# Layer 0's attention begins with heads 0 and 1, later key and query tiles run beside head 0, and values stay in SBUF

## The chip, the cores and the metric

The kernel runs on one core of one Trainium2 chip, as one launch. The metric is the device time of the launch in microseconds (us). The engines are named as the profile names them: PE is TensorE (PEld its weight loads), DVE is VectorE, ACT is ScalarE, POOL is GpSimd and SP is SyncE, which issues all DMA transfers of this kernel in one queue. SBUF is the memory on the core, DRAM the memory beside it.

## The reference

One inference step of a two-layer network over 1024 latent and 128 context tokens, 1024 channels wide. Layer 0 is what this case is about; layer 1 (a neighbourhood attention) and the feed-forward parts follow.

```python
def mla_split(h, w_in, ...):
    a_in, q_lat, kv_lat, k_rope = split(h @ w_in, (512, 768, 896), axis=-1)
    q = (rms_norm(q_lat, q_lora_norm) @ w_q_up).reshape(B, S, 8, 96)    # 64 plain + 32 rotary channels a head
    q = rms_norm(q, mla_q_norm)                                          # over the 96 channels of each head
    ckv = rms_norm(kv_lat, kv_lora_norm)
    return a_in, q, ckv, k_rope

def mla_keys_values(ckv, k_rope, w_kv_up, mla_k_norm):
    kv = (ckv @ w_kv_up).reshape(B, L, 8, 64 + 64)
    k_nope, v = kv[..., :64], kv[..., 64:]
    k = concatenate([k_nope, broadcast_to(k_rope, every head)], axis=-1)
    return rms_norm(k, mla_k_norm), v

def pool_mla_latent(h, ckv_ctx, krope_ctx, ...):
    ...
    q, k = rope_tail(q), concatenate([rope_tail(k_lat), k_ctx], axis=1)
    v = concatenate([v_lat, v_ctx], axis=1)                              # 1024 + 128 keys
    attn = softmax(q @ k.T * 96 ** -0.5) @ v                             # 8 heads
    return concatenate([pool_mixer(a_in, w_pool, pool_scale), attn], axis=-1) @ w_out
```

Context tokens run the same projections and attend to context tokens alone (`pool_mla_context`). `pool_mixer` subtracts each channel from a windowed mean and multiplies four groups of 128 channels by a 128x128 matrix each. Beside this a modulation is computed for each layer, silu(c) @ w_ada + b_ada, 6 x 1024 values from a 1024 x 6144 matrix.

## The kernel before, in words

**Precision.** An f32 product is made of three matmuls: each operand is split into a high half (a cast on ACT) and a low half (the operand less its high half), and low·high, high·low and high·high add up in one PSUM tile. So each tile of keys or queries exists as a high and a low tile.

**Stages of layer 0 around the change.** The in-projection and the query chunks (`query_chunk`, three pieces of 384 tokens) leave raw keys and queries of all heads as channel-by-token tiles: four tiles of plain channels with two heads each (tiles 0 to 3) and two of rotary channels with four heads each (tiles 4 and 5). `key_tile(t)` and `query_tile(t)` finish a tile: PE spreads the norm's factors over the partitions (`bcast`, L682 and L683, two matmuls with 8 rows into PSUM tile `ps_b`), DVE multiplies with them (L758 and L779 among others), and `split_store` casts the high half `fh` on ACT, subtracts on POOL for the low half (L691) and stores both to DRAM (`qdn`, `qdr`, `kdn`, `kdr`). Tiles run in the order 4, 0, 5, 1, 2, 3. A head needs one plain and one rotary tile: head 0 needs 0 and 4, heads 2 and 3 need 1 and 4, heads 4 to 7 need 5 with 2 or 3. `load_qk(h)` brings a head's high halves back as 96-row tiles `qh` and `kh`, `load_rest(h)` the low halves `ql` and `kl` and the head's values.

After the tiles comes one block: `max_units` of heads 0 and 1, woven with `value_gen` (values, stored to DRAM as `vd`, ten steps), `context_gen0` (attention of the context tokens) and `mix_gen` (the pooling mixer, L826 its vector part `pl`).

**Maxima.** The softmax subtracts a maximum for each query. `max_units(h)` computes the scores once in low precision: 24 matmuls of 96x384 (L1034), each reduced by DVE (L1035). Then `put_max` reduces the 24 columns to 8 (L1016), transposes them on PE (`ps_mt`, L1020), and sends the row through DRAM: `row` to `mrow` and `mrow` to row 96 of `qh`. Row 96 of `kh` holds ones, so that the third matmul of a score (L1074, 97 rows) subtracts the maximum by itself. Of a head's scores only L1074 needs the maxima; the first two (L1070, L1073) don't.

**The heads.** Each head has two halves of 512 queries, each with nine key tiles: three matmuls into `ps_st`, an exponential on ACT into `p`, and the product with the values (`ps_pv`, L1077), one key tile's scores being issued ahead of an earlier one's product. At a half's end DVE copies the result out (L1001). Beside head h run the maxima of head h + 2, and the modulation (`ada_gen`: a load of `wada`, a reduction with `silu` on DVE, L200) as background work that the head calls twice a half, from head 0 on.

**What sets the order.** Python generators are interleaved by `weave`, which always takes the next step of the generator that is least far along by its weight; the numbers beside the generators are these weights. A scheduler behind it then sorts each engine's instructions by its own estimate of when each can run, under data dependences and one added rule (`LAG`): a score isn't started before the maximum that lies four maxima back in the program. Each engine runs its list strictly in order, so an instruction that waits holds all behind it. SBUF is given out in slots by a small allocator (`S`); PSUM tiles come from three tags, with three buffers for `ps_st`, three shared by maxima, broadcasts and small work, two for the products.

## Time and profile before

| | |
|---|---|
| median of 3 runs | 3011.77 us (3011.28 to 3014.54) |
| the profiled execution's own time | 3018.45 us |
| its span in the trace | 3016.6 us |
| PE busy | 2914.8 us, 97% |
| PEld busy | 2612.8 us, 87% |
| DVE busy | 2149.4 us, 71% |
| ACT busy | 1331.9 us, 44% |
| POOL busy | 306.9 us, 10% |
| DMA | 372 MB, mean 123 GB/s |
| share of the chain that ended last | PE 80%, DVE 6%, DMA 6%, issue 5% |

The times below are from the span's start. The stretch that the change touches runs from the tiles, at about 231 us, to the end of head 7, at 576.2 us. In the profile's rows a number after `L` is the line, the letters before it the engine, then operation, output and inputs. Rows of a group end with the time busy and the mean of one in ns, then the idle time ahead of them and what ended it. Rows of the timeline begin with the start and the length in us. `SPq` is a transfer, at the time at which SP issued it. PEclk is the clock that PE was granted, as a share of the full one, and a windows row gives it after the engines.

### The profile page before, as it was taken

The page shows a single profiled execution, that of the slowest core. Times are in us where ns is not written, and L with a number is a line of the kernel's source. Part 1 is how long each engine was busy: PE and PEld are TensorE (multiplying, and loading weights), DVE is VectorE, ACT ScalarE, POOL GpSimd, SP SyncE. Part 2 cuts the span into 40 slices and gives each one's busy share as a digit, 9 for nine tenths or more (in the row PEclk, how much of TensorE's full clock was granted, in tenths as well). Part 3 has the DMA queues.
Part 4 walks back from the last instruction along what each step waited for, and adds up shares of the span by engine and source line. Part 5 has one row for each costly group of instructions (what it writes and reads, how often), then busy time and mean ns, then how long its engine had stood idle before and what let it go on. Part 6 is the DMA issues. An engine that isn't in the chain of part 4 may idle for free.

```text
span 3016.6 us, 46513 instructions
## 1 busy us (share of the span) xinstructions
PE 2914.8 (97%) x18302; PEld 2612.8 (87%) x18302; DVE 2149.4 (71%) x3921; ACT 1331.9 (44%) x2177; POOL 306.9 (10%) x210
## 2 busy tenths in 40 slices
PE   7998899999999999999999999998989999999999
...
PEclk9996899999999999999999999998999999999999
...
GB/s 234 169 62 306 212 61 50 77 76 86 99 84 85 105 133 147 85 99 80 173 187 223 126 146 208 185 240 155 101 29 98 79 97 85 116 100 78 98 76 87
DMA packets 148268, 372.37 MB, mean 123 GB/s; under 512 B 14225, under 2 KB 67073, under 8 KB 148050
## 3 DMA queue, kind: packets, MB, share of 16 engines
...
## 4 chain that ended last, share of the span: by engine, by line
PE 80%; DVE 6%; DMA 6%; issue 5%; ACT 2%; POOL 1%; SPq 0%; DVEq 0%; POOLq 0%; ACTq 0%
PE ps L452 9%; PE ps L454 9%; PE ps L453 9%; PE ps L422 8%; PE ps L424 8%; PE ps L423 8%; PE ps_n L335 2%; PE ps_n L336 2%; PE ps_n L337 2%; PE ps_pv L1329 2%; PE ps_o L335 1%; PE ps_o L336 1%; PE ps_o L337 1%; PE ps_pv L1077 1%; PE ps_v L1353 1%
## 5 line engine op out<-in xcount | busy, mean ns | idle before, releaser
L452 PE MATMUL ps<-ml,wh 128*128 128x288 f32 x2048 | 592.3, 296 | 10.3 <-DVE ml L441 7.8
L453 PE MATMUL ps<-mh,wl 128*128 128x288 f32 x2048 | 601.3, 295 | 0.0
L454 PE MATMUL ps<-mh,wh 128*128 128x288 f32 x2048 | 597.0, 295 | 0.0
L422 PE MATMUL ps<-bl,wh 128*128 128x288 f32 x1792 | 532.8, 298 | 13.3 <-DVE bl L353 10.3
L423 PE MATMUL ps<-bh,wl 128*128 128x288 f32 x1792 | 529.7, 296 | 0.0
L424 PE MATMUL ps<-bh,wh 128*128 128x288 f32 x1792 | 528.2, 295 | 0.0
L452 PEld LDWEIGHTS ps<-ml,wh 128*128 128x128 f32 x2048 | 381.5, 188 | 11.3 <-DVE ml L441 8.3
L453 PEld LDWEIGHTS ps<-mh,wl 128*128 128x128 f32 x2048 | 385.5, 188 | 0.0
L454 PEld LDWEIGHTS ps<-mh,wh 128*128 128x128 f32 x2048 | 383.6, 188 | 0.1
L458 DVE SCALAR_TENSOR_TENSOR x<-ps,ada,x 128x288 f32<-128x288 f32 (+2 forms) x640 | 270.0, 451 | 119.1 <-PE ps L454 117.8
L422 PEld LDWEIGHTS ps<-bl,wh 128*128 128x128 f32 x1792 | 336.8, 188 | 16.7 <-issue 11.5
L424 PEld LDWEIGHTS ps<-bh,wh 128*128 128x128 f32 x1792 | 338.4, 189 | 0.0
L423 PEld LDWEIGHTS ps<-bh,wl 128*128 128x128 f32 x1792 | 337.5, 188 | 0.2
L395 ACT CAST wh<-s 128x512 fp32r<-128x512 f32 x256 | 146.1, 618 | 305.8 <-PE ps L454 217.1
L160 ACT CAST wh<-wr 128x1024 fp32r<-128x1024 f32 x188 | 196.9, 1050 | 176.4 <-PE ps L424 79.9
L200 DVE CUSTOM_DVE_ANT_0 trash<-wada,silu 128x1024 bf16<-128x1024 f32 x160 | 203.2, 1270 | 28.0 <-DMA wada<-in_wada0t 16.4
L161 DVE TENSOR_TENSOR wl<-wr,wh 128x1024 fp32r<-128x1024 f32 x144 | 179.6, 1251 | 46.6 <-ACT wh L160 46.5
L395 ACT CAST wh<-wr 128x1024 fp32r<-128x1024 f32 (+1 forms) x128 | 106.9, 835 | 220.5 <-PE ps L454 155.4
L161 POOL TENSOR_TENSOR wl<-wr,wh 128x1024 fp32r<-128x1024 f32 x44 | 119.3, 2718 | 701.9 <-ACT wh L160 686.2
L396 DVE TENSOR_TENSOR wl<-s,wh 128x512 fp32r<-128x512 f32 x232 | 157.1, 710 | 3.5 <-ACT wh L395 1.2
L1278 DVE CUSTOM_DVE_ANT_0 trash<-ps_m,ta 128x512 bf16<-128x512 f32 (+1 forms) x128 | 83.4, 651 | 100.7 <-PE ps_m L1276 91.9
L1035 DVE TENSOR_REDUCE stat<-ps_m 128x1 f32<-128x384 f32 x192 | 99.3, 551 | 77.8 <-PE ps_m L1034 77.4
...
## 6 DMA issues: line engine op xcount, KB each, us to landing
wr<-in_w SPq DMA_DIRECT2D x256, 512.0 KB
...
```

The source lines that it names most:

```text
L160: nc.scalar.copy(hi, r)
L161: (nc.gpsimd if e else nc.vector).tensor_sub(lo, r, hi)
L200: nc.vector.tensor_tensor_reduce(trash, r[:, :D], silu[i][:, :D], scale=1.0, scalar=0.0, op0=ALU.mult, op1=ALU.add, accum_out=a)
L395: nc.scalar.copy(h, src)
L396: (nc.gpsimd if j in EDGE and min(ps) in EDGE_POOL else nc.vector).tensor_sub(l, src, h)
L422: nc.tensor.matmul(ps, wh[:, a], hl[:, b], start=k == 0, stop=False)
L423: nc.tensor.matmul(ps, wl[:, a], hh[:, b], start=False, stop=False)
L424: nc.tensor.matmul(ps, wh[:, a], hh[:, b], start=False, stop=k == 3)
L452: nc.tensor.matmul(ps, wh, hl, start=kk == 0, stop=False)
L453: nc.tensor.matmul(ps, wl, hh, start=False, stop=False)
L454: nc.tensor.matmul(ps, wh, hh, start=False, stop=kk == 3)
L458: nc.vector.scalar_tensor_tensor(x[m][:, a:b], ps[:, a - ch * HC:b - ch * HC], g, x[m][:, a:b], op0=ALU.mult, op1=ALU.add)
```

## The change

Three things are changed, and the diff below shows them, with unchanged lines left out at "...".

**Values.** `vd` and its loads are gone. `value_gen` writes each token tile's values, in two pieces by ACT, straight into six SBUF tiles `vt` (three for heads 0 to 3, three for 4 to 7) in the layout that the product reads, whose columns of ones POOL writes once. `head_values0` gives the piece for a key tile and head.

**Order ahead of head 0.** Key and query tiles became generators that take the engine of their subtraction: DVE for tiles 4 and 0, POOL as before for the others. Tiles 4 and 0 run first, then head 0's loads, then a block of head 0's maxima, the values and tile 1, then head 1's high loads. Head 0 starts behind it.

**Beside the heads.** Head 0 runs beside head 1's maxima and `rest_gen`: tiles 5 and 2, the low loads of head 1, the high loads of head 2, tile 3. Head 1 runs beside head 2's maxima and the mixer, head 2 beside head 3's maxima and the context tokens, each later head beside the maxima of the next one, not of the one after it. The modulation starts with head 2 and is called three times a half. Copies of the context's results move to heads 4 and 6.

```diff
--- before.py
+++ after.py
@@ -524,7 +524,6 @@
 
     qd_n, qd_r = [DR(f"qdn{i}", [4, P, NS]) for i in range(2)], [DR(f"qdr{i}", [2, P, NS]) for i in range(2)]
     kd_n, kd_r = [DR(f"kdn{i}", [4, P, TOK]) for i in range(2)], [DR(f"kdr{i}", [2, P, TOK]) for i in range(2)]
-    vd0 = DR("vd0", [9, P, 768], F32)
 
 
...
@@ -684,11 +683,11 @@
 
...
-    def split_store(raw, ncols, dst, i):
+    def split_store(raw, ncols, dst, i, eng):
         hi, lo = S.alloc("fh", F32R), raw.bitcast(F32R)
         c = slice(0, ncols)
         nc.scalar.copy(hi[:, c], raw[:, c])
-        nc.gpsimd.tensor_sub(lo[:, c], raw[:, c], hi[:, c])
+        eng.tensor_sub(lo[:, c], raw[:, c], hi[:, c])
...
         S.free(hi)
@@ -746,7 +745,7 @@
                 nc.vector.tensor_add(tq[t - 2][:, cs], tq[t - 2][:, cs], sw)
...
-    def key_tile(t):
+    def key_tile(t, eng):
         raw = tk[t] if t < 4 else S.alloc("kro")
         for ch in range(NCH):
             ps = PS("ps_b", "pb")[:, :CH]
@@ -758,16 +757,18 @@
                     nc.vector.scalar_tensor_tensor(o, raw[:, a:b], V("kn_nope"), pp_, op0=ALU.mult, op1=ALU.mult)
                 else:
                     nc.vector.tensor_mul(o, krr[:, a:b], pp_)
+            yield
...
         if t < 4:
             nc.vector.scalar_tensor_tensor(raw[:, NS:], tkc[:, t * P:t * P + P], V("kn_nope"), ps, op0=ALU.mult, op1=ALU.mult)
         else:
             nc.vector.tensor_mul(raw[:, NS:], kr4c, ps)
-        split_store(raw, TOK, kd_n if t < 4 else kd_r, t if t < 4 else t - 4)
+        split_store(raw, TOK, kd_n if t < 4 else kd_r, t if t < 4 else t - 4, eng)
         S.free(raw)
-
-    def query_tile(t):
+        yield
+
+    def query_tile(t, eng):
         raw = tq[t]
         for ch in range(NCH):
             ps = PS("ps_b", "pb")[:, :CH]
@@ -779,24 +780,35 @@
                     nc.vector.scalar_tensor_tensor(o, raw[:, a:b], V("qn_nope"), pp_, op0=ALU.mult, op1=ALU.mult)
                 else:
                     nc.vector.tensor_mul(o, raw[:, a:b], pp_)
-        split_store(raw, NS, qd_n if t < 4 else qd_r, t if t < 4 else t - 4)
+            yield
+        split_store(raw, NS, qd_n if t < 4 else qd_r, t if t < 4 else t - 4, eng)
         S.free(raw)
+        yield
+
+    def tile_gen(t, eng):
+        yield from key_tile(t, eng)
+        yield from query_tile(t, eng)
 
     for ch in range(NCH):
         query_chunk(ch)
     S.free(*[t for p in qlat for t in p], rc, rs, nt)
     for t in (4, 0):
-        key_tile(t)
-        query_tile(t)
-    for t in (5, 1, 2, 3):
-        key_tile(t)
-        query_tile(t)
-    S.free(krr, *rk8, bcs)
+        run(tile_gen(t, nc.vector))
+
 
 
     vp = S.alloc("vp")
+    vt0 = [[S.alloc(f"vt{q}{i}") for i in range(3)] for q in range(2)]
+    v40 = [[t.rearrange("p (a e f) -> p a e f", e=3, f=64) for t in q] for q in vt0]
+
+    def head_values0(t, h):
+        o = t % 3 * 384 + h % 4 // 2 * 192 + h % 2 * 64
+        return vt0[h // 4][t // 3][:, o:o + P]
 
     def value_gen():
+        for q in v40:
+            for t in q:
+                nc.gpsimd.memset(t[:, :, 1], 1.0)
         for tt in range(10):
             ps = PS("ps_v")
             if tt < 9:
@@ -809,12 +821,12 @@
             if tt == 8:
                 nc.scalar.copy(vp[:, :512], ps)
             else:
-                vs = S.alloc("vst")
-                place_values(vs[:, :768], ps)
-                dma(vd0[min(tt, 8)], vs[:, :768])
-                S.free(vs)
+                t = min(tt, 8)
+                for q in range(2):
+                    nc.scalar.copy(v40[q][t // 3][:, t % 3 * 2:t % 3 * 2 + 2, 0:3:2],
+                                   ps[:, q * 256:q * 256 + 256].rearrange("p (g e f) -> p g e f", e=2, f=64))
             yield
-        S.free(*ckv, small)
+        S.free(*ckv)
...
@@ -977,14 +989,13 @@
         return qh, kh
 
     def load_rest(h):
-        ql, kl, v = S.alloc("ql", F32R), S.alloc("kl", F32R), S.alloc("v")
+        ql, kl = S.alloc("ql", F32R), S.alloc("kl", F32R)
         n0, r0 = 64 * (h % 2), 32 * (h % 4)
         dma(ql[0:64, :NS], qd_n[1][h // 2, n0:n0 + 64, :])
         dma(ql[64:96, :NS], qd_r[1][h // 4, r0:r0 + 32, :])
         dma(kl[0:64, :], kd_n[1][h // 2, n0:n0 + 64, :])
         dma(kl[64:96, :], kd_r[1][h // 4, r0:r0 + 32, :])
-        load_pv(vd0, h, v)
-        return ql, kl, v
+        return ql, kl
 
 
...
@@ -1055,8 +1066,7 @@
...
     def attend_units(h, qk, rest, opair, den):
-        (qh, kh), (ql, kl, vv) = qk, rest
-        v = vv.rearrange("p (t f) -> p t f", t=9)
+        (qh, kh), (ql, kl) = qk, rest
...
         for half in range(2):
...
@@ -1074,14 +1084,14 @@
...
                 nc.scalar.activation(p_, ps, AF.Exp, scale=scale0)
-                nc.tensor.matmul(po, v[:, kt, :], p_, start=kt == 0, stop=kt == 8)
+                nc.tensor.matmul(po, head_values0(kt, h), p_, start=kt == 0, stop=kt == 8)
...
                     held = None
                 if kt == 6:
                     later()
-                if kt in (2, 6):
+                if kt in (1, 4, 7):
                     background()
                 yield
             finish_values(64 * (h % 2), half, po, opair, den, half and h % 2)
@@ -1089,29 +1099,54 @@
 
     background(10 ** 6)
     S.free(*silu)
-    qks = {0: load_qk(0), 1: load_qk(1)}
-    weave((chain(max_units(0, qks[0]), max_units(1, qks[1])), 50), (chain(value_gen(), context_gen0()), 17),
-          (mix_gen(), 13))
-    rest = load_rest(0)
-    silu_load()
-    bg.append(chain(ada_gen(0, range(16 + 8 * NEARLY, 48)), free_silu()))
+    qks = {0: load_qk(0)}
+    rest = {0: load_rest(0)}
+    weave((max_units(0, qks[0]), 25), (value_gen(), 10), (tile_gen(1, nc.gpsimd), 7))
+    qks[1] = load_qk(1)
+
+
+    def rest_gen():
+        yield from tile_gen(5, nc.gpsimd)
+        yield from tile_gen(2, nc.gpsimd)
+        rest[1] = load_rest(1)
+        qks[2] = load_qk(2)
+        yield
+        yield from tile_gen(3, nc.gpsimd)
+        S.free(krr, *rk8, bcs, small)
+
     opairs = []
     for h in range(8):
         if h % 2 == 0:
             op, den = S.alloc(f"o{h}"), S.alloc("den")
             opairs.append(op)
-            nc.vector.tensor_copy(op[:, NS:], oat[:, (h // 2) * P:(h // 2) * P + P])
-        gs = [(attend_units(h, qks[h], rest, op, den), 19)]
+        if h == 2:
+            silu_load()
+            bg.append(chain(ada_gen(0, range(16 + 8 * NEARLY, 48)), free_silu()))
+        if h == 4:
+            for i in range(3):
+                nc.vector.tensor_copy(opairs[i][:, NS:], oat[:, i * P:i * P + P])
+        if h == 6:
+            nc.vector.tensor_copy(op[:, NS:], oat[:, 3 * P:4 * P])
+            S.free(oat)
+        gs = [(attend_units(h, qks[h], rest[h], op, den), 19)]
+        if 0 < h < 7:
+            rest[h + 1] = load_rest(h + 1)
+        if 0 < h < 6:
+            qks[h + 2] = load_qk(h + 2)
         if h < 7:
-            nrest = load_rest(h + 1)
-        if h < 6:
-            qks[h + 2] = load_qk(h + 2)
-            gs.append((max_units(h + 2, qks[h + 2]), 27))
+            gs.append((max_units(h + 1, qks[h + 1]), 31))
+        if h == 0:
+            gs.append((rest_gen(), 24))
+        elif h == 1:
+            gs.append((mix_gen(), 14))
+        elif h == 2:
+            gs.append((context_gen0(), 8))
         weave(*gs)
-        S.free(*qks[h], *rest)
-        rest = nrest
+        S.free(*qks[h], *rest[h])
+        if h == 3:
+            S.free(*vt0[0])
+    S.free(*vt0[1])
     later(2)
-    S.free(oat)
 
 
...
```

The rows that follow are the programs' instruction lists. Lines of the changed kernel have other numbers: L1045 and L1046 are the maxima and their reductions, L1080, L1083 and L1084 the three matmuls of a score, L1087 the product with the values, L1031 the transpose of the maxima, L757, L764, L780 and L782 the tiles' multiplications, L690 the subtraction for the low half.

First DVE at tiles 4 and 0. `tq_204` is the query of tile 4, `tk_192` and `tq_200` key and query of tile 0, `kro` the key of tile 5. Before:

```order
L758 SCALAR_TENSOR_TENSOR pp_190_1438<-tk_192_1459,vec,ps_b 128x128
L764 SCALAR_TENSOR_TENSOR tk_192_1459<-small_1417,vec,ps_b 128x128
L779 SCALAR_TENSOR_TENSOR tq_200_1626<-tq_200_1626,vec,ps_b 128x384 x2
L779 SCALAR_TENSOR_TENSOR tq_200_1626<-tq_200_1626,vec,ps_b 128x256
L779 SCALAR_TENSOR_TENSOR pp_189_1437<-tq_200_1626,vec,ps_b 128x128
L760 TENSOR_TENSOR kro_2004<-krr_1420,ps_b 128x384 x2
L760 TENSOR_TENSOR kro_2004<-krr_1420,ps_b 128x256
```

And in the changed kernel:

```order
L690 TENSOR_TENSOR tq_204_1629<-tq_204_1629,fh_1958 128x1024
L757 SCALAR_TENSOR_TENSOR tk_192_1458<-tk_192_1458,vec,ps_b 128x256
L757 SCALAR_TENSOR_TENSOR pp_190_1437<-tk_192_1458,vec,ps_b 128x128
L780 SCALAR_TENSOR_TENSOR tq_200_1625<-tq_200_1625,vec,ps_b 128x384
L764 SCALAR_TENSOR_TENSOR tk_192_1458<-small_1416,vec,ps_b 128x128
L780 SCALAR_TENSOR_TENSOR tq_200_1625<-tq_200_1625,vec,ps_b 128x384
L690 TENSOR_TENSOR tk_192_1458<-tk_192_1458,fh_1980 128x1152
L780 SCALAR_TENSOR_TENSOR tq_200_1625<-tq_200_1625,vec,ps_b 128x256
L780 SCALAR_TENSOR_TENSOR pp_189_1436<-tq_200_1625,vec,ps_b 128x128
L690 TENSOR_TENSOR tq_200_1625<-tq_200_1625,fh_1998 128x1024
L1046 TENSOR_REDUCE stat<-ps_m 128x1 x3
L757 SCALAR_TENSOR_TENSOR tk_193_1459<-tk_193_1459,vec,ps_b 128x384
```

The subtraction of tile 4's query stands in front of tile 0's last key products, that of tile 0's key between its query products, and head 0's reductions follow on tile 0 where tile 5 stood.

Second PE at the boundary of heads 0 and 1 in the changed kernel (`qh_2213`, `kh_2214`, `ql_2456` and `kl_2457` are head 1's, `qh_2462` and `kh_2463` head 2's):

```order
L1087 MATMUL ps_pv<-p_2488,vt_228_2005 128x512
L1080 MATMUL ps_st<-qh_2213,kl_2457 128x512
L1083 MATMUL ps_st<-ql_2456,kh_2214 128x512
L1031 MATMUL ps_mt<-ident,stat 8x128
L681 MATMUL ps_b<-rkh_1463,bcs_1407 128x384
...
L1087 MATMUL ps_pv<-p_2488,vt_229_2006 128x512
L1087 MATMUL ps_pv<-p_2526,vt_229_2006 128x512 x2
L681 MATMUL ps_b<-rkh_1463,bcs_1407 128x384
L682 MATMUL ps_b<-rkl_1464,bcs_1407 128x384
...
L682 MATMUL ps_b<-rkl_1464,bcs_1407 128x384
L1084 MATMUL ps_st<-qh_2213,kh_2214 128x512
```

The transpose of head 1's maxima stands three products and some broadcasts ahead of the first L1084 of head 1, which needs them after their way through DRAM. At the boundary of heads 6 and 7 (`qh_3634` and `kh_3635` are head 7's) there are fewer rows between:

```order
L1087 MATMUL ps_pv<-p_4064,vt_232_2009 128x512
L1080 MATMUL ps_st<-qh_3634,kl_3857 128x512
L1083 MATMUL ps_st<-ql_3856,kh_3635 128x512
L1031 MATMUL ps_mt<-ident,stat 8x128
L1087 MATMUL ps_pv<-p_4064,vt_232_2009 128x512
L1080 MATMUL ps_st<-qh_3634,kl_3857 128x512
L1083 MATMUL ps_st<-ql_3856,kh_3635 128x512
L1084 MATMUL ps_st<-qh_3634,kh_3635 128x512 x3
L1087 MATMUL ps_pv<-p_4081,vt_230_2007 128x512
```

Before, the same transpose of head 7's maxima stood among the scores of head 6 (`qh_3506`), with 14 of the head's 18 scores still to be finished behind it:

```order
L1074 MATMUL ps_st<-qh_3506,kh_3507 128x512
L1020 MATMUL ps_mt<-ident,stat 8x128
L1077 MATMUL ps_pv<-p_3966,v_3732 128x512
L1070 MATMUL ps_st<-qh_3506,kl_3731 128x512
L1073 MATMUL ps_st<-ql_3730,kh_3507 128x512
```

Third SP around head 7's maxima. `x` are loads of the residual for the out-projection, 0.56 MB each. Before, both transfers of the maxima came ahead of them (`qh_3738` is head 7's there):

```order
L113 DMA mrow_2172<-row 8x128
L113 DMA qh_3738<-mrow_2172 1x1024
L113 DMA x_562_4240<-in_xT 128x1152
L113 DMA x_559_4237<-in_xT 128x1152
```

In the changed kernel the loads stand around and between them:

```order
L113 DMA x_543_4217<-in_xT 128x1152
L113 DMA mrow_2016<-row 8x128
L113 DMA x_540_4214<-in_xT 128x1152
L113 DMA qh_3634<-mrow_2016 1x1024
L113 DMA x_545_4219<-in_xT 128x1152
```

One load of x lies between the store of the maxima and their way back into row 96.

## The prediction

> **What bounds the kernel now.** First the row of slices on the page: TensorE (PE) is busy almost everywhere, and its granted clock falls in two slices, the fourth and fifth (226 to 377 us).

> ```profile
> PE   7998899999999999999999999998989999999999
> PEclk9996899999999999999999999998999999999999
> ```

> Then the windows view of those slices, cut where the work changes: the last query chunk, the key and query tiles, the block of maxima, values, mixer and context, the first half of head 0, and all other halves of the attention.

> ```profile
> core 0: us, PE busy (x) PEld busy (x) DVE busy (x) ACT busy (x) POOL busy (x), PEclk, DMA share, GB/s
> 231.00:257.60 26.60, 22.69 (x72) 17.16 (x72) 20.79 (x48) 13.69 (x13) 22.76 (x10) 0.50 0.89 330
> 257.60:318.90 61.30, 48.18 (x168) 35.15 (x169) 43.77 (x83) 21.29 (x47) 13.22 (x14) 0.69 0.98 298
> 318.90:344.20 25.30, 23.35 (x72) 14.37 (x70) 20.64 (x39) 7.76 (x13) 0.00 (x0) 0.90 0.74 217
> 344.20:576.20 232.00, 231.39 (x813) 149.31 (x812) 112.27 (x207) 93.33 (x158) 7.13 (x3) 1.00 0.28 81
> ```

> From 231 to 318.9 nothing runs at its own speed: PE has half clock, then 0.69, and the DMA engines are full. From 344.2 PE is never idle, at full clock. So the change can win before 318.9 and can only lose behind it. Third the timeline, for the marks: first row maxima, first full score of head 0, and copies of finished halves.

> ```profile
> 257.66 5.25 PE L1034 MATMUL ps_m<-kh,qh 96*128 96x384 f32 x11 [3.86 <-DMA kh<-kdr]
> 318.89 0.63 PE L1074 MATMUL ps_st<-qh,kh 97*128 97x512 f32 x1
> 421.01 0.68 DVE L1001 COPY o<-ps_pv 64x512 f32<-64x512 f32 x1 [1.36 <-PE ps_pv L1077]
> 437.21 0.69 DVE L1001 COPY o<-ps_pv 64x512 f32<-64x512 f32 x1 [0.99 <-PE ps_pv L1077]
> 532.17 0.68 DVE L1001 COPY o<-ps_pv 64x512 f32<-64x512 f32 x1 [4.57 <-PE ps_pv L1077]
> 546.21 0.68 DVE L1001 COPY o<-ps_pv 64x512 f32<-64x512 f32 x1 [13.36 <-PE ps_pv L1077]
> ```

> A half with 12 maxima takes 16.20 us, one without 14.04, so a maximum costs PE 0.18.

> **Term 1, the start of head 0: 46.4 us earlier.** Tiles 4 and 0 now subtract on DVE, ahead of head 0's loads.

> ```profile
> 236.86 1.04 ACT L690 CAST fh<-tq 128x1024 fp32r<-128x1024 f32 x1 [0.67 <-DVE tq L779]
> 237.93 0.32 SPq L113 DMA_DIRECT2D qdn<-fh  x1
> 249.05 0.51 SPq L113 DMA_DIRECT2D qh<-qdn  x1
> 262.09 2.35 DVE L826 TENSOR_TENSOR pl<-pooled,ph 128x1152 fp32r<-128x1152 f32 x1
> 275.96 1.34 DVE L826 TENSOR_TENSOR pl<-pooled,ph 128x1152 fp32r<-128x1152 f32 x1
> 271.30 4.74 DVE L1035 TENSOR_REDUCE stat<-ps_m 128x1 f32<-128x384 f32 x10 [1.40 <-PE ps_m L1034]
> 241.19 1.72 DVE L758 SCALAR_TENSOR_TENSOR tk<-tk,vec,ps_b 128x384 f32<-128x384 f32 x3
> 277.22 0.17 DVE L1016 TENSOR_REDUCE stat<-stat 128x8 f32<-128x24 f32 x1
> ```

> Two subtractions, 1.34 and 1.19 (by width), stand on DVE before tile 0's query is done, and DVE waits for a cast before each: 1.1 and 0.7. With 0.2 of handover that is 4.5, so the query's high half is stored from 242.4, not 237.9. Before, 19.7 us lay between that store and the first maximum, since the load was issued 11 us after it, behind stores of tiles 5 and 1. Those are gone from ahead of it; I take 7 (two trips of 2 to 3 us, and 1.5 MB at the window's 330 GB/s beside them). First maximum: 249.5. Then 24 reductions at 0.474 (11.4) with 3.3 us of tile 1's products on the same engine; the block of before took 257.7 to 277.2 for 11.4 plus 3.6 of mixer, so some 4 idle, of which I take 2.3: 266.5. Then the maxima's trip through memory:

> ```profile
> 285.77 0.54 SPq L113 DMA_DIRECT2D mrow<-row  x1
> 299.37 0.24 SPq L113 DMA_DIRECT2D qh<-mrow  x1
> 347.48 0.30 SPq L113 DMA_DIRECT2D mrow<-row  x1
> 349.90 0.25 SPq L113 DMA_DIRECT2D qh<-mrow  x1
> 454.95 0.27 SPq L113 DMA_DIRECT2D mrow<-row  x1
> 456.14 0.21 SPq L113 DMA_DIRECT2D qh<-mrow  x1
> ```

> The first of its two transfers takes 1.2 in quiet, 2.4 under load, 13.6 in a jam. Two under load with transpose and cast (0.6) and a store of tile 1 ahead: 6. First full score at 272.5 instead of 318.9. Ends: 265 (no idling, quick trip) and 288 (nothing gained on the loads, jammed trip).

> **Term 2, work that now runs inside the attention: +20.8.** Before, it ran ahead of 318.9.

> ```profile
> 270.05 0.34 PE L337 MATMUL ps_p<-ph,wh 128*128 128x384 f32 x1
> 270.23 0.40 PE L804 MATMUL ps_v<-wl,ckh 128*128 128x512 f32 x1
> L682 PE MATMUL ps_b<-rkh,bcs 8*128 8x384 f32 x33 | 18.2, 621 | 5.0 <-DVE rkh L678 5.0
> L952 PE MATMUL ps_po<-ctxw,vp 128*64 128x128 f32 x16 | 2.2, 435 | 0.0
> L922 PE MATMUL ps_t<-ident,ctxw 128*128 128x128 f32 x8 | 2.2, 426 | 0.0
> L946 PE MATMUL ps_s<-ctxqk,ctxqk 96*128 96x128 f32 x16 | 2.1, 274 | 0.0
> ```

> A 384-column matmul takes 0.18 of PE's time at full clock (start to start). Maxima: 34 more, 6.1. Mixer: 36 matmuls, 6.3. Tiles 5, 2 and 3: about 34 such matmuls, less some already run in the wait for the first score, 5.4. Context: the three groups' 6.5, about half at full clock, 3.0. The tiles' vector work (some 4.3 us each by the L758 row) fits: head 0 has 28 us of DVE work beside 39 of PE. Ends: 16 and 26 (half clock on part of it).

> **Term 3, new waits: +23.** Before, a head's maxima were ready a whole head ahead. In the new order the last of them stands at the boundary of heads 0 and 1, and of 4 to 7, a few matmuls before the first score that needs them. PE work that covers the trip there, counted from the order: 4.2 us at head 1, 5.1 at head 5, 2.4 at head 6, 1.3 at head 7. Behind the score on PE stands everything else. At head 1 the trip is under load (8 with a context store between its two parts): 4, and 3 more since head 1's low keys are loaded behind tile 2's query store: 7. Head 5: 0. Head 6, trip of 4: 1.5. Head 7, where a 0.56 MB load of x stands between the two transfers on SP: 4.5. What a wait does to the clock:

> ```profile
> 332.72 0.90 PE L1034 MATMUL ps_m<-kh,qh 96*128 96x384 f32 x2 [1.81 <-DVE stat L1035]
> 335.42 0.63 PE L1074 MATMUL ps_st<-qh,kh 97*128 97x512 f32 x1
> 338.15 0.40 PE L1074 MATMUL ps_st<-qh,kh 97*128 97x512 f32 x1
> L200 DVE CUSTOM_DVE_ANT_0 trash<-wada,silu 128x1024 bf16<-128x1024 f32 x32 | 39.0, 1219 | 13.4 <-DMA wada<-in_wada0t 13.0
> ```

> After 1.81 us of waiting matmuls run at half speed for some 4.5 us, which costs about 2; for two boundaries I take 2 in all, since the others are short. [...]

> The 32 modulation reductions (L200) move from heads 0 and 1 to heads 2 and 3. Between the ends of head 1 and of head 3's first half DVE holds 30 of them (36.6), 39 maxima (18.5), three half copies, a division and context steps (7.3): 62.4. PE has three halves (42.1), 39 maxima (7.0) and the context (3.0): 52.1. Of the 10 excess PE runs ahead by three score buffers and a tail, and 6.5 stay. Loads that L200 waits for (13.0 before, with full DMA engines) I take at 1.5. Sum 7 + 1.5 + 4.5 + 2 + 6.5 + 1.5 = 23. Ends: 8 and 38.

> **Term 4, what the old start lost: 7 back.** Head 0's first half took 25.3 from the first full score, for 14.0 and 1.9 of maxima: 9 lost to clock and DVE. I keep 2 of it, as PE starts cold. Ends 0 and 9.

> **At nothing:** the 3.1 MB of stored values and eight loads of them (off the path at 81 GB/s; without that cover the 0.56 MB would be 2 us a head), the value copies in two pieces on ScalarE (busy 93 of 232), and three background calls a half for two. Eight subtractions stay on GpSimd beside head 0. [...]

> **Sum.** 46.4 - 20.8 - 23 + 7 = 9.6 us gained. The profiled execution took 3018.45 (span 3016.6 and 1.85 around it), 6.7 over the median of 3011.77. On the median: **3002 us**, with its own range 2994 to 3009.

> **Rivals.** (a) The waits are covered: DVE and the queue run ahead at the boundaries, and term 3 is at its low end, 8. For it: in quiet the trip is 1.2; against: the order leaves 1.3 and 2.4 us of cover. Gain 24.6: 2987. Chance 0.18. (b) The start isn't moved as far: the loads of head 0 still queue behind stores at a DMA share of 0.89, the first maximum stays near 257.7, and the gain falls by 8.2 to 1.4: 3010. For it: six stores and a weight load are still ahead on SP; against: four stores fewer. This is also the case in which the overlap does not do what it says. Chance 0.22. (c) Slower: the exposed trip. With one head's lead gone, each boundary pays it; jammed at head 1 (15.6 less 4.2, and 3 for the low keys), 10 at head 7 behind the x loads, 4 at head 6 and 3 at head 5, with 1.5 of clock each, it is 37.4 instead of 15. The point where it decides is 24.6 at the boundaries. Loss 12.8: 3025. For it: the 13.6 row; against: at 454.95 and later the queue is quiet. Chance 0.15. The forecast has 0.45.

> About 0.2% (6 us) is what a measurement can tell from no change. Faster by over that: most of the forecast (0.40) and (a), 0.58. Within it: the rest of the forecast and most of (b), 0.25. Slower: (c) and a little of (b), 0.17. The range runs from below (a)'s price to short of (c)'s: 2985 to 3020.

> **What would show it.** The first maximum near 249.5 and the first full score near 272.5 (term 1); heads 0 and 1 at some 39 us each at clock near 1 (term 2); PE waiting before the first full score of heads 1, 6 and 7, and DVE full in heads 2 and 3 (term 3). A first score after 285, or waits above 10 us at a boundary, would make the forecast wrong; so would heads 2 and 3 at 32 us.

## The result, and the profile after

The change makes the kernel slower. The median went from 3011.53 us (8 runs) to 3032.3 us (8 runs), a ratio of 1.0061 with a 95% interval of [1.0044, 1.0077]. The forecast was 3002, so both its sign and its range were wrong. The profiled execution of the changed kernel took 3024.94 us (span 3023.2), against 3018.45 (3016.6) before.

The row of slices on the page, as in the prediction (slices of 75.6 us; the fourth is 227 to 302 us), and the shares of the chain of waits:

```profile
PE   7997999899999999999999999998989999999999
PEclk9996999999999999999999989989999999999999
...
PE 86%; DVE 6%; DMA 5%; ACT 2%; issue 1%; POOL 1%; SPq 0%; DVEq 0%; ACTq 0%; POOLq 0%
```

By the row of the clock the changed kernel looks better: one slow slice where there were two. Only the 8 of PE's eighth slice (529 to 605) hints at a loss, since a slice is wider than a wait. The windows view, cut at the ends of heads, shows it. First the changed kernel from 226 us, with the start of head 0 at 278.3 and then one row a head:

```profile
core 0: us, PE busy (x) PEld busy (x) DVE busy (x) ACT busy (x) POOL busy (x), PEclk, DMA share, GB/s
226.00:278.30 52.30, 35.53 (x96) 21.66 (x96) 32.11 (x58) 13.84 (x28) 12.60 (x10) 0.62 0.56 176
278.30:325.00 46.70, 45.93 (x142) 25.66 (x140) 21.18 (x46) 19.14 (x28) 10.49 (x5) 0.91 0.44 152
325.00:375.00 50.00, 47.37 (x176) 33.72 (x177) 28.11 (x49) 23.26 (x39) 6.92 (x3) 0.93 0.52 147
375.00:424.00 49.00, 43.41 (x163) 28.39 (x162) 45.47 (x88) 18.77 (x43) 2.77 (x1) 0.90 0.55 162
424.00:454.70 30.70, 30.70 (x107) 19.55 (x106) 27.05 (x52) 12.04 (x21) 0.00 (x0) 1.00 0.56 160
...
550.60:591.30 40.70, 33.68 (x116) 21.14 (x115) 11.75 (x21) 11.69 (x20) 0.00 (x0) 0.87 0.24 88
```

Then the kernel before, cut in the same way (its head 0 starts at 318.9):

```profile
226.00:318.90 92.90, 70.95 (x241) 52.32 (x241) 69.37 (x137) 36.55 (x63) 39.60 (x25) 0.64 0.93 300
318.90:357.50 38.60, 36.65 (x119) 23.07 (x118) 33.52 (x62) 13.02 (x23) 0.00 (x0) 0.94 0.66 202
357.50:388.60 31.10, 30.49 (x105) 19.27 (x104) 19.36 (x39) 11.55 (x20) 0.00 (x0) 1.00 0.39 111
388.60:420.90 32.30, 32.30 (x117) 21.20 (x116) 16.69 (x30) 13.83 (x23) 2.38 (x1) 1.00 0.28 71
...
546.20:576.20 30.00, 30.00 (x111) 19.24 (x111) 14.06 (x25) 10.72 (x18) 0.00 (x0) 1.00 0.29 115
```

Head 0 starts 40.6 us earlier, as the change says. But its eight heads take 313.0 us instead of 257.3, so head 7 ends 15.1 us later, at 591.3 instead of 576.2. Four heads hold the loss: 0, 1, 2 and 7. Heads 3 to 6 together take 126.6, against 125.1 before.

The 55.7 us that the heads grew by fall into three parts. PE waits 16.4 us between its instructions instead of 2.6: 13.9 before rounding. It is at half clock for 35.8 us instead of 4.9, and half of the time that it works at half clock is lost. In 7.5 of the 35.8 it stands still and the time is a wait already: 5.1 ahead of head 7's first full score, 2.0 in head 1, 0.35 in head 2. So the clock costs half of 28.3 less half of 4.9: 11.7. A window around head 7's stretch shows the overlap, with PE busy for 4.95 of 10 us at a clock of 0.50:

```profile
553.00:563.00 10.00, 4.95 (x9) 2.98 (x10) 0.00 (x0) 1.66 (x4) 0.00 (x0) 0.50 0.37 148
```

What is left is 30.1 us of PE's work, most of which formerly ran ahead of head 0. The waits view of PE for the changed kernel, 225 to 600 us (total, times, longest), says for what it waits:

```profile
PE ps_m L1045 <- DMA qh<-qdn: 12.9, 1, 12.9
PE ps_st L1084 <- DMA qh<-mrow: 7.0, 1, 7.0
PE ps_mt L1031 <- DVE stat L1027: 4.9, 2, 4.8
...
PE ps_p L335 <- DVE pl L838: 2.5, 1, 2.5
```

The 12.9 are ahead of the first maximum and belong to the start. The other three lie in heads 7, 2 and 1.

The spans of the two profiled executions differ by 6.6, not 15.1, because layer 1's attention happened to take 291.0 us in the one of after and 302.8 in the one of before, in waits for its own maxima's rows. Repeats gave 297.0 and 293.6 for it, so that is spread. The medians differ by 20.8. The heads are therefore the measure below, and the medians the verdict.

### The profile page after: what moved, and what is told of

It is laid out like the page before. It is cut to its first block, busy times and chain, and to the rows that moved or that the text cites. A ratio compares the mean times of both kernels' runs of the same rounds, so it can differ in the third digit from the quotient of the medians.

```text
span 3023.2 us, 46473 instructions
## 1 busy us (share of the span) xinstructions
PE 2915.9 (96%) x18302; PEld 2604.3 (86%) x18302; DVE 2146.6 (71%) x3925; ACT 1329.7 (44%) x2186; POOL 296.9 (10%) x203
## 4 chain that ended last, share of the span: by engine, by line
PE 86%; DVE 6%; DMA 5%; ACT 2%; issue 1%; POOL 1%; SPq 0%; DVEq 0%; ACTq 0%; POOLq 0%
PE ps L452 9%; PE ps L454 9%; PE ps L453 9%; PE ps L422 8%; PE ps L424 8%; PE ps L423 8%; PE ps_pv L1087 4%; PE ps_pv L1364 2%; PE ps_n L337 2%; PE ps_n L336 2%; PE ps_n L335 2%; PE ps_o L335 1%; PE ps_o L336 1%; PE ps_o L337 1%; PE ps_v L1388 1%; PE ps_m L1045 1%
## 5 line engine op out<-in xcount | busy, mean ns | idle before, releaser
L422 PE MATMUL ps<-bl,wh 128*128 128x288 f32 x1792 | 532.5, 297 | 13.1 <-DVE bl L353 10.2
L452 PEld LDWEIGHTS ps<-ml,wh 128*128 128x128 f32 x2048 | 382.3, 189 | 10.9 <-DVE ml L441 8.3
L200 DVE CUSTOM_DVE_ANT_0 trash<-wada,silu 128x1024 bf16<-128x1024 f32 x160 | 203.9, 1274 | 17.0 <-DMA wada<-in_wada 7.1
L161 DVE TENSOR_TENSOR wl<-wr,wh 128x1024 fp32r<-128x1024 f32 x144 | 179.9, 1253 | 46.7 <-ACT wh L160 46.7
L1046 DVE TENSOR_REDUCE stat<-ps_m 128x1 f32<-128x384 f32 x192 | 99.3, 552 | 79.8 <-PE ps_m L1045 79.2
```

The costliest lines, as they stand in the source:

```text
L161: (nc.gpsimd if e else nc.vector).tensor_sub(lo, r, hi)
L200: nc.vector.tensor_tensor_reduce(trash, r[:, :D], silu[i][:, :D], scale=1.0, scalar=0.0, op0=ALU.mult, op1=ALU.add, accum_out=a)
L422: nc.tensor.matmul(ps, wh[:, a], hl[:, b], start=k == 0, stop=False)
L452: nc.tensor.matmul(ps, wh, hl, start=kk == 0, stop=False)
```

## The experiments

All runs in one table. "Start" is the first full score of head 0. The heads run from there, or from the end of the head before, to the copy of the second half. "Wait" and "half" are PE's idle time and its time at half clock in the eight heads. All are in us and from the timelines of the profiled executions. The ratio is to the kernel before, with its 95% interval. a_again, b_again and each e-run are explained below.

| run | start | heads 0 to 7 | sum | wait | half | ratio |
|---|---|---|---|---|---|---|
| before | 318.9 | 38.6 31.1 32.3 32.3 32.3 32.3 28.2 30.0 | 257.3 | 2.6 | 5 | 1 |
| b_again | 315.2 | 38.7 32.3 32.3 32.3 32.3 32.3 28.2 30.0 | 258.5 | 4.0 | 3 | 3009.05 us, one run |
| after | 278.3 | 46.7 50.0 49.0 30.7 30.4 32.6 32.9 40.7 | 313.0 | 16.4 | 36 | 1.0061 [1.0044, 1.0077] |
| a_again | 280.2 | 50.1 50.4 49.0 30.7 30.4 32.6 32.9 40.8 | 316.8 | 16.6 | 47 | 1.0050 [1.0030, 1.0070] |
| e1_x_held | 279.7 | 47.1 51.0 48.8 30.7 30.4 32.7 32.9 33.2 | 306.7 | 12.3 | 26 | 1.0036 [1.0019, 1.0053] |
| e2_mod_late | 278.4 | 46.6 50.2 37.5 32.5 31.2 38.0 34.1 40.4 | 310.4 | 14.7 | 29 | 1.0077 [1.0048, 1.0105] |
| e3_x_mod | 277.8 | 47.0 51.7 46.3 32.1 30.7 30.4 35.1 33.6 | 307.0 | 13.0 | 26 | 1.0048 [1.0030, 1.0067] |
| e4_x_mod_mix | 279.7 | 46.4 42.7 50.3 39.8 29.8 31.0 35.1 31.9 | 307.1 | 9.9 | 33 | 1.0040 [1.0020, 1.0059] |
| e5_values_only | 323.3 | 36.7 32.3 32.3 32.3 32.3 32.3 28.2 30.1 | 256.7 | 1.8 | 2 | 1.0035 [1.0018, 1.0052] |
| e6_pool_sub | 281.1 | 49.1 52.7 49.6 31.7 31.2 31.4 32.9 40.2 | 318.8 | 19.5 | 41 | 1.0075 [1.0047, 1.0102] |
| e7_even | 277.2 | 52.1 48.7 43.6 32.2 34.0 34.2 35.5 32.0 | 312.4 | 18.7 | 25 | 1.0080 [1.0060, 1.0099] |
| e8_even_spread | 276.5 | 42.3 53.0 58.3 41.2 30.0 34.2 35.5 31.9 | 326.4 | 25.2 | 45 | 1.0103 [1.0083, 1.0123] |
| e9_bcast_more | 278.9 | 50.1 50.8 49.6 31.0 31.2 30.9 32.9 39.9 | 316.4 | 15.8 | 32 | 3043.11 us, one run |
| e10_values_dram | 279.9 | 44.8 57.1 48.6 29.5 30.3 32.6 32.9 41.1 | 316.9 | 19.0 | 35 | 1.0074 [1.0052, 1.0097] |
| e11_mix_first | 280.5 | 47.8 46.0 48.8 30.2 33.3 33.2 33.0 33.2 | 305.5 | 12.2 | 35 | 1.0055 [1.0034, 1.0076] |
| e12_mix_mod1 | 282.0 | 46.2 39.4 61.9 28.3 30.9 33.3 32.9 33.3 | 306.2 | 14.2 | 32 | 1.0061 [1.0039, 1.0083] |
| e13_pv_rule | 280.6 | 53.1 45.4 48.5 32.0 31.1 32.4 28.9 32.0 | 303.4 | 10.1 | 32 | 1.0065 [1.0043, 1.0088] |
| e14_all | 281.0 | 54.6 35.3 32.4 45.3 32.3 32.3 31.8 32.0 | 296.1 | 8.4 | 27 | 1.0002 [0.9981, 1.0023] |
| e15_more | 280.7 | 45.0 38.5 34.3 39.8 32.4 32.3 32.1 31.7 | 286.1 | 6.5 | 6 | 0.9982 [0.9967, 0.9996] |
| e16_rules | 277.6 | 55.6 46.5 45.8 34.1 33.4 32.3 32.0 31.8 | 311.6 | 17.8 | 31 | 1.0070 [1.0056, 1.0085] |

**a_again and b_again** are the two kernels unchanged, as the yardstick.

> The changed kernel once more, for its ratio beside the others and for a second trace. In the first trace head 7 ends at 591.3 us, 15.1 later than before, while the rest of the program took 8.5 less than in the trace of before, most of it (12) in layer 1's attention, whose code the change leaves alone. Theory: all of the loss lies ahead of 591 and the 12 us are a spread from execution to execution; then this trace has head 7's end within 1 us of 591.3, layer 1's attention may be anywhere between 285 and 302 us, and the ratio to before is 1.004 to 1.008. Rival: the change itself shortens or lengthens layer 1's attention; then this trace shows the same 288 us, within 2, as the first.

> The kernel before once more, for a second trace. Theory: head 7 ends within 1 us of 576.2 and layer 1's attention differs from the 299.8 us of the first trace by several us. Rival (layer 1 depends on the change): 299.8 within 2.

The stages come back: the start to 2 to 4 us, heads 2 to 7 to 0.1, head 1 to 0.4 in after and 1.2 in before, but head 0 of after has 46.7 and 50.1, with 8 and 16 us at half clock. But head 7 ends at 597.1 and 573.8, not within the 1 us of 591.3 and 576.2 that was expected. By the two traces of each kernel the loss there is 19.2 on average, near the 20.8 of the medians. A difference of less than 4 us in the sum is not read below.

**e1_x_held** takes head 7's wait away: the load of x that stood ahead of the maxima's second transfer is issued behind it.

```diff
-        dma(x[k], I["xT"][k])
+        after(dma(x[k], I["xT"][k]), trips[7])      # trips[h]: the transfer mrow -> qh of head h
```

> The changed kernel with one thing added: the eight loads of x are ordered on SP behind the last transfer of head 7's maxima. Theory: PE's 7.0 us of waiting at the boundary of heads 6 and 7 and the half clock of 10 us behind it (5 lost) come from the x load between the two transfers; with it gone the wait is 2 to 3 us, the clock stays up, and the attention ends 8 to 10 us earlier, at 581 to 583, for a ratio of about 1.003. Rival: the trip through DRAM itself is too long for the 1.3 us of cover; then the wait stays at 5 or more and the end moves by less than 3.

The transfers as SP issued them in the changed kernel, and the score that waited:

```profile
550.02 0.29 SPq L113 DMA_DIRECT2D mrow<-row  x1
550.59 0.60 SPq L113 DMA_DIRECT2D x<-in_xT  x1
556.66 0.24 SPq L113 DMA_DIRECT2D qh<-mrow  x1
558.05 1.65 PE L1084 MATMUL ps_st<-qh,kh 97*128 97x512 f32 x3 [7.02 <-DMA qh<-mrow]
```

In e1 the same score stands like this:

```profile
555.14 0.96 PE L1086 MATMUL ps_st<-qh,kh 97*128 97x512 f32 x3 [1.59 <-DMA qh<-mrow]
```

Head 7 falls from 40.7 to 33.2. PE waits 5.2 us less in it, and the half clock (553 to 563 in the changed kernel, of which PE works 5) is gone: 5.2 and half of 5 make 7.7, where 7.5 is measured. The end of head 7 is at 586.3, not at the 581 to 583 that was expected. So the exposed trip at head 7, with the x load in it, cost 7.5 us, half of the 15.1 at the end of head 7.

**e2_mod_late, e3_x_mod, e4_x_mod_mix** go at the DVE queue of head 2 and the mixer of head 1. e2 starts the modulation with head 4 and calls it twice a half. e3 is e1 with each modulation reduction ordered behind the maximum's reduction that precedes it in the program. e4 is e3 with the mixer beside head 3.

```diff
-        if h == 2:                       # e2
+        if h == 4:
-                if kt in (1, 4, 7):
+                if kt in (2, 6):
+                if mxr and layer == 0:   # e3, q: the reduction L200, mxr: the reductions L1046
+                    after(q, mxr[-1])
-        elif h == 1:                     # e4
-            gs.append((mix_gen(), 14))
+        elif h == 3:
+            gs.append((chain(iter(range(4)), mix_gen()), 17))
```

> The changed kernel with the modulation started at head 4 instead of 2 and called twice a half instead of three times. Theory: in heads 2 and 3 DVE had more work than PE; without the modulation's 36.6 us PE's 5.4 us of waiting at head 3's transpose and the half clock behind it (5 lost) vanish, head 2 falls from 49 to about 38 us and head 3 stays at 31; in heads 4 and 5 DVE has some 61 us of work beside 63 of PE, so at most 4 come back there. Attention ends 7 to 11 us earlier. Rival: the surplus only moves, and heads 4 and 5 lose what head 2 gains (end within 2 us of 591); or the context's reductions are what holds DVE, and head 2 stays above 45.

> The x loads held as in e1_x_held, and one more rule: each reduction of the modulation (L200) stands on DVE behind the reduction of a maximum that precedes it in the program, so that it can no longer be moved ahead; start at head 2 and three calls a half stay. In the changed kernel's order they were all in heads 2 and 3; now about five or six stand in each of heads 2 to 7. Theory (in head 2 the bunched modulation, not the amount of DVE work as such, holds the last reductions and the transpose): the 5.1 us wait in head 2 and the half clock of 10 us behind it go, head 2 falls from 49 to 38 to 40 us, heads 4 to 7 lose less than 3 together, and from the first full score to the end of head 7 it is 296 to 299 us for 306.6 in e1_x_held; ratio to before about 1.000. Rival from e2_mod_late (whichever head takes the modulation pays what head 2 gains): 303 or more.

> As e3_x_mod, and the mixer runs beside head 3, from some four key tiles on, instead of beside head 1 from its start. Theory: at the boundary of heads 0 and 1 PE waits 2.5 us for the mixer's first vector part, which stands behind the copy of head 0's half on DVE, and the clock halves for 7 us or more; with the mixer gone from there both go, head 1 falls from 50 to about 38 us and head 3 rises by about 7 (36 products at 0.2), so the attention ends another 5 to 6 us earlier than in e3_x_mod; ratio about 0.998. Rival: the clock falls at that boundary for another reason (the many 8-row broadcasts just ahead), and the gain is 2.5 at most.

What PE waited for in head 2 of the changed kernel is a transpose of maxima, and DVE's list shows what stands ahead of its input L1027:

```profile
389.92 1.21 DVE L200 CUSTOM_DVE_ANT_0 trash<-wada,silu 128x1024 bf16<-128x1024 f32 x1
391.06 1.22 DVE L1058 SCALAR_TENSOR_TENSOR o<-o,den 128x1024 f32<-128x1024 f32 x1
392.28 0.14 DVE L1027 TENSOR_REDUCE stat<-stat 128x8 f32<-128x24 f32 x1
392.48 0.36 PE L1031 MATMUL ps_mt<-ident,stat 128*8 128x128 f32 x1 [4.79 <-DVE stat L1027]
```

DVE is busy 45.47 of head 2's 49.0. e2 empties it and head 2 falls to 37.5, so the modulation is the cause there. But head 5 then takes 38.0 with a wait of 3.0 and 7 us at half clock, and the sum changes by only 2.6. The rule of e3 alone leaves head 2 at 46.3, where 38 to 40 was expected. e4 takes the mixer out of head 1, which falls by 9.0 against e3. Head 3, which has the mixer now, grows by 7.7, and head 2 by 4.0. Against e1, which they contain, e3 and e4 change the sum by 0.3 and 0.4. Each cause is real where it stands, but what leaves one head comes back in another.

**e5_values_only** is the kernel before with the values in SBUF alone. **e10_values_dram** is the changed kernel with the values back in DRAM.

```diff
-                vs = S.alloc("vst")
-                place_values(vs[:, :768], ps)
-                dma(vd0[min(tt, 8)], vs[:, :768])
-                S.free(vs)
+                for q in range(2):       # e5; e10 is the same in reverse
+                    nc.scalar.copy(v40[q][t // 3][:, ...], ps[...])
```

> The kernel before with one part of the change alone: values stay in SBUF, and no load of them per head. Theory: costs and gains nothing along the heads (below 0.2% of the whole), since PE never waited for a load of values; the block ahead of head 0 may gain 2 to 5 us, as 3.5 MB of stores and the first load leave a stretch in which the DMA engines are full. Ratio 0.998 to 1.000. Rival: two ScalarE copies in place of one delay the exponentials: slower by over 0.2%.

> The changed kernel with its first part undone: values go to DRAM and come back for each head, the rest stays. Theory (prediction: at nothing): head lengths as in the changed kernel within 2 us each, ratio 1.003 to 1.007 as there. Rival (six of 36 slots held for the values make others wait, as in e5_values_only, where PE waited 16.8 us for a slot): the heads get 5 us or more shorter in sum. Other rival: stores and loads of values crowd the queue at head 0, and the first full score comes 2 us or more later.

Alone, the values cost 0.35%, where a gain of up to 0.2% was expected. Their six tiles hold slots, and the rows fit a mixer's cast that waits for a store of keys to give one back:

```profile
266.21 1.15 ACT L833 CAST ph<-pooled 128x1152 fp32r<-128x1152 f32 x1 [12.01 <-DMA kdn<-tk]
268.86 0.69 PE L335 MATMUL ps_p<-pl,wh 128*128 128x384 f32 x1 [16.80 <-DVE pl L834]
```

The start goes from 318.9 and 315.2 to 323.3, and the heads stay as they were. That is 4.4 to 8.1 us of the 11.1 between the medians, and where the rest is lost was not found. In the changed order the mixer has left that place, and in e10 the sum is that of the changed kernel within the spread, though single heads differ by more than the 2 us expected (head 1 takes 57.1). So no part of the loss is shown to come from the values, though "at nothing" was wrong for them in the old order.

**e6_pool_sub** gives the subtractions of tiles 4 and 0 back to GpSimd.

```diff
-        run(tile_gen(t, nc.vector))
+        run(tile_gen(t, nc.gpsimd))
```

> The changed kernel with the subtractions of tiles 4 and 0 back on POOL. By the prediction's first term they cost 4.5 us on DVE ahead of the store of head 0's query; then the first maximum comes 2 to 4 us earlier than 254 and so does the first full score. Rival: DVE waits for casts and products there anyway and the loads of head 0 wait in the queue for the low halves, which POOL delivers at twice the time; then the first maximum moves by less than 1 us, or is later, by up to 4.

The first maximum comes at 256.9 instead of 254.1 and 256.0, and the start at 281.1 instead of 278.3 and 280.2. Within the spread that is the same: neither a gain nor the cost of 4.5 us that term 1 gave to the two subtractions shows.

**e7_even and e8_even_spread** order work inside a head. In e7 (on e3) each maximum's matmul goes behind the score that precedes it in the program. e8 adds tile 3 beside head 1 and the mixer beside head 3.

```diff
+                if scs:                                  # e7; scs: the matmuls L1084
+                    after(mxi[-1], scs[-1])
-            gs.append((rest_gen(), 24))                  # e8, rest_gen without tile 3
+            gs.append((rest_gen(), 17))
+            gs.append((tile3_gen(), 9))                  # h == 1; mix_gen at h == 3 as in e4
```

> As e3_x_mod, and each maximum stands on PE behind the score that precedes it in the program. In e3_x_mod head 3's 24 maxima all ran in the first 17 us of head 2, with seven modulation reductions (which follow them), a division and the context's reductions on DVE, and PE stood 4.8 us before a transpose whose result is needed 30 us later. Theory (bunching): spread over the head, the maxima leave DVE room, that wait and the half clock of 7 us behind it go, head 2 falls from 46 to 40 us or less, and from the first full score to the end of head 7 it is 298 to 301 us for 306.9. Rival (the time is the price of mixed matmuls on PE, wherever they stand): 305 or more, and the boundaries wait more, since the last maxima now end later.

> As e7_even, with tile 3 beside head 1 instead of head 0, and the mixer beside head 3, from some four key tiles on, instead of head 1. Theory: fewer 8-row broadcasts in a row and no wait for the mixer's first vector part at the boundary of heads 0 and 1, so that the half clock around 318 to 335 us goes or halves; from the first full score to the end 290 to 295 us, ratio 0.996 to 0.999. Rival from e4_x_mod_mix (what leaves one head returns in another): 298 or more, ratio above 1.000.

Both are worse than e3. With maxima spread evenly their last one comes late, and e7's PE waits for their row at five places, 7.5 us in all. In e8 it waits 7.2 for head 1's low keys, up to 5.1 for a row of maxima and 4.7 for the context's tiles. Evenness without an earlier end of the maxima makes new waits.

**e9_bcast_more** prices the matmuls with 8 rows. For tiles 5, 2 and 3 the first of the two broadcast matmuls of 21 pairs is issued twice, with the same result.

> The changed kernel with the first 8-row broadcast of each pair issued twice for tiles 5, 2 and 3 (21 matmuls of 384 columns more, the result unchanged). It measures the disputed price by itself. By the prediction's 0.18 head 0 grows by 3.8 us; by 0.25, which the changed kernel's head 0 seems to show, by 5.3; if the clock counts 8-row matmuls as idle, a window or two of half clock (3.4 us each) come on top, and head 0 and the start of head 1 grow by 7 or more.

The sum is 316.4 against 313.0 and 316.8, and PE has 32 us of half clock, against 36 and 47, so the 7 us or more of that theory do not come. Where the doubled ones stand in a row, each further one takes 0.17 to 0.18. But the theory that 8-row matmuls pull the clock down is not refuted. PE is never idle in head 0 of e9, and yet from 300.6 to 304.0 the clock is at half, right behind six of these matmuls, where both traces of the changed kernel have full clock. Four products of values take 3.51 there, and 1.98 in the row further below:

```profile
300.04 0.33 PE L684 MATMUL ps_b<-rkl,bcs 8*128 8x384 f32 x1
300.31 3.51 PE L1089 MATMUL ps_pv<-p,vt 128*128 128x512 f32 x4
```

In the changed kernel a lone pair between a score and a product of values takes 0.55 from start to start, in place of 0.36:

```profile
289.13 0.40 PE L1084 MATMUL ps_st<-qh,kh 97*128 97x512 f32 x1
289.46 0.44 PE L681 MATMUL ps_b<-rkh,bcs 8*128 8x384 f32 x1
289.75 0.33 PE L682 MATMUL ps_b<-rkl,bcs 8*128 8x384 f32 x1
290.01 1.98 PE L1087 MATMUL ps_pv<-p,vt 128*128 128x512 f32 x4
```

So the price seems to lie in the change of kind (0.29 for the first, 0.26 to the next product), not in the rows.

**e11_mix_first, e12_mix_mod1, e13_pv_rule.** e11 is e1 with values and mixer run ahead of head 0's maxima. e12 adds the modulation from head 1 on. e13 is e11 with one rule: the scores of a key tile are not started before the product of values that lies two back.

```diff
+    run(value_gen())                                     # e11, ahead of head 0's maxima
+    run(mix_gen())                                       # and none beside head 1
-        if h == 2:                                       # e12: the modulation
+        if h == 1:
+                if len(pvs) >= 2:                        # e13; st: a score's first matmul
+                    after(st, pvs[-2])
```

> As e1_x_held, with the mixer taken out of head 1 and put on PE between the values and head 0's first maximum, where PE waits 12.4 us for head 0's loads in the changed kernel. Theory (the price is paid where PE has other work, and the low clock at the start comes from that idle time): 36 products at half clock fill some 12 us that were idle, so the first full score stays within 3 us of 279.7, the clock is up earlier than 286 us, head 0 gets 2 to 4 us shorter and head 1 falls from 51 to 40 to 43 (as in e4_x_mod_mix); from the first full score to the end 293 to 297 us for 306.7, ratio 0.999 to 1.001. Rival (what leaves one head returns in another, as in e4, e7 and e8): 303 or more, or a first full score after 286.

> As e11_mix_first, with the modulation started at head 1 instead of head 2, on a DVE that the mixer has left. Theory: in head 2 the 5.6 us wait and the 10 us of half clock go or halve, since some of the modulation's 36.6 us on DVE lie in head 1; head 2 falls from 49 to 39 to 43 us, head 1 grows by at most 3; from the first full score to the end 285 to 291 us, ratio 0.996 to 0.999: faster than both kernels. Rival from e2_mod_late: head 1 pays what head 2 gains, and the sum stays within 3 us of e11_mix_first.

> As e11_mix_first, and one more rule of order on PE: the scores of a key tile stand behind the product with the values of the second key tile before it. In e11_mix_first PE ran back to back from 333.6 to 349 us at half clock, with scores and maxima alone (96 rows) and no product with the values (128 rows); the clock came back when the products did, and head 1 took 46.0 us where its work at full clock is some 36. Theory (the clock stays low while only such products run): interleaved, the half clock in head 1 falls from 17 to 7 us or less and head 1 to 39 to 42 us; the sum of the heads 299 to 302. Rival: the low clock follows from the waits at the boundary alone, and stays at 14 or more.

The start hardly moves (280.5, 279.7 in e1): the mixer fits into the wait for the first loads. Yet the sums stay at 303 to 306. In e12 head 1 falls to 39.4 and head 2 rises to 61.9, with some 9 us of waits. In e11 a stretch of half clock, from 332.7 to 349.7, has no wait in most of it. Its windows:

```profile
333.00:340.00 7.00, 6.41 (x17) 5.12 (x18) 3.09 (x7) 1.28 (x3) 3.69 (x2) 0.50 0.99 351
340.00:350.00 10.00, 10.00 (x28) 7.60 (x27) 6.38 (x13) 3.88 (x7) 0.00 (x0) 0.51 0.53 145
350.00:360.00 10.00, 10.00 (x29) 5.14 (x28) 1.38 (x3) 1.54 (x3) 0.00 (x0) 1.00 0.46 127
```

The scheduler had put the maxima and scores of that stretch together, without products of values between them. I took that for the cause of the slow clock. In e13 head 1 stays at 45.4 and its half clock shrinks only from 17 to 10. That does not decide it, since the rule put another bunch in place of the first: 18 maxima in a row, from 334.1 to 342.3, without a product of values. The last 15 of them:

```profile
335.13 7.19 PE L1051 MATMUL ps_m<-kh,qh 96*128 96x384 f32 x15 [0.30 <-DVE stat L1054]
```

The half clock of e13 begins in that bunch, at 340.1.

**e14_all, e15_more, e16_rules.** e14 puts the rules and the placing together: e13, maxima ordered behind scores, modulation behind maxima, maxima with more weight, the modulation from head 1 and the context beside head 3. e15 adds tile 3 beside head 1, head 1's low loads ahead of tile 2, the modulation from head 2, and the context's transposes three steps later. e16 has e14's rules, but values, mixer, modulation and context where the change put them.

```diff
-            gs.append((max_units(h + 1, qks[h + 1]), 31))   # e14
+            gs.append((max_units(h + 1, qks[h + 1]), 40))
-        elif h == 2:                                        # e14: context_gen0
+        elif h == 3:
-        yield from tile_gen(2, nc.gpsimd)                   # e15, in rest_gen
         rest[1] = load_rest(1)
+        yield from tile_gen(2, nc.gpsimd)
-            gs.append((context_gen0(), 8))                  # e15
+            gs.append((context_gen0(), 13))
```

> As e13_pv_rule, with the maxima and the modulation held to the program's places as in e7_even and e3_x_mod, maxima at weight 40 instead of 31 (so that the last transpose stands three to five key tiles ahead of the boundary), the modulation from head 1 on and the context beside head 3. Theory: with each source of waits seen so far removed (x loads, mixer, bunched maxima, bunched modulation, boundaries), heads 1 and 2 take 36 to 39 us, the others 32 to 36, and the sum is 285 to 292 us, ratio 0.995 to 0.999: faster than both kernels. Rival (the sum is held by DVE's and PE's work together and comes out near 306 whatever the order): 302 or more, ratio above 1.003.

> As e14_all, with tile 3 beside head 1 instead of head 0, head 1's low loads ahead of tile 2, the modulation from head 2 on, and the context's transposes three steps later in the program and held behind the score ahead of them. In e14_all head 0 took 54.6 us with 16 of half clock, after eight pairs of broadcasts in a row, and head 3 took 45.3 with a 3.0 us wait for the context's last vector step and 10 of half clock; the other heads took 32 to 35. Theory: head 0 falls to 45 to 48, head 1 grows to 37 to 39, head 3 falls to 36 to 39; the sum is 281 to 286 us for 296.1, ratio 0.994 to 0.998: faster than both kernels. Rival from e8_even_spread (what leaves head 0 comes back in head 1): 292 or more.

> The changed kernel with the rules of order of e14_all alone (x loads behind head 7's maxima, products with the values at most one key tile behind, maxima and modulation at their places in the program, maxima at weight 40), while mixer, modulation and context stay where the change put them. It tells how much of e14_all's gain is the order of the lists and how much the moved work. Theory (the scheduler's bunching is the larger part of what the forecast missed): the sum of the heads is 295 to 301 us for 313 to 317, ratio 1.000 to 1.003. Rival (the places of mixer, modulation and context decide): 304 or more.

e14 is at 1.0002, no faster than the kernel before, with a sum of 296.1 where 285 to 292 was expected. e15 is at 0.9982 [0.9967, 0.9996], 3008.43 us against 3012.02: faster than both kernels, by little. Its windows show why, heads 0 to 4:

```profile
280.70:325.70 45.00, 43.19 (x141) 26.07 (x141) 19.64 (x43) 14.50 (x23) 9.08 (x4) 0.93 0.44 146
325.70:364.20 38.50, 37.87 (x133) 23.44 (x132) 19.31 (x40) 15.68 (x25) 7.37 (x3) 1.00 0.50 162
364.20:398.50 34.30, 33.21 (x116) 21.11 (x115) 22.60 (x42) 13.34 (x23) 2.36 (x1) 1.00 0.63 176
398.50:438.30 39.80, 36.85 (x156) 24.41 (x155) 24.12 (x50) 17.19 (x42) 0.00 (x0) 1.00 0.27 75
438.30:470.70 32.40, 32.40 (x117) 21.30 (x116) 22.91 (x44) 13.97 (x23) 2.37 (x1) 1.00 0.53 137
```

No head but the first is below full clock, and DVE is at most 71% busy in these rows, where it had 93% in head 2 of the changed kernel. Head 7 ends at 566.8 us, 9.4 before the one of the kernel before. What e15 saves is waits and clock. The sum less the waits and less half of the time worked at half clock is PE's work. It was 282.4 in the changed kernel and 252.3 before, and is still 276.5. In the eleven traces with the changed kernel's work beside the heads it lies between 281.5 and 284.1, whatever the order, in the five with the mixer ahead of head 0 (e11 to e15) between 275.4 and 278.6, and in e9, with 21 matmuls more, at 287.0. So order changes waits and clock, and only moved work changes the rest. With the rules alone, e16 has 311.6 and 1.007: the rules don't do it without the moved work, which was e16's question. The moved mixer and modulation without the rules (e12) don't either.

## Why the prediction was wrong

On the profiled executions the forecast was 9.6 us gained, and at the end of head 7 there were 15.1 lost, 24.7 apart. The start misses by 5.8 and the work by 9.3. The waits come out 7.1 better than forecast (13.9 for 21). The clock misses by 16.7: 2 lost behind waits and 7 back from the old start were forecast, 5 gained in all, and 11.7 were lost. This is the step that failed most: without it the end of head 7 would have come 1.6 us earlier than before.

- **Term 1, the start: 46.4 forecast, 40.6 measured.** Tile 0's query went out at 243.2, 0.8 later than said. What failed is the 7 us from there to the first maximum. They were 10.9: the query's load was issued 5.5 us after its store, behind stores, an 0.5 MB weight load and the keys' loads.

```profile
243.19 0.32 SPq L113 DMA_DIRECT2D qdn<-fh  x1
244.00 0.33 SPq L113 DMA_DIRECT2D wr<-in_wout  x1
...
248.71 0.45 SPq L113 DMA_DIRECT2D qh<-qdn  x1
254.09 1.30 PE L1045 MATMUL ps_m<-kh,qh 96*128 96x384 f32 x3 [12.91 <-DMA qh<-qdn]
273.21 0.27 SPq L113 DMA_DIRECT2D mrow<-row  x1
274.41 0.21 SPq L113 DMA_DIRECT2D qh<-mrow  x1
278.26 1.48 PE L1084 MATMUL ps_st<-qh,kh 97*128 97x512 f32 x3
```

  The block of maxima (254.1 to 272.3, 18.2 for 17) and the trip (6.0 for 6) were right. Rival (b), a start that isn't moved as far, was right in part.

- **Term 2, the work: 20.8 forecast, 30.1 measured.** 0.18 for a side matmul holds in the quiet heads, where 25 of them cost 4.2 to 4.5 us. The 55 of head 0 cost 0.25 each and the 80 of head 1 0.21 (the head less waits, half of what it works at half clock, and 28.1 for scores and products). That pairs of broadcasts, mixer products and transposes stand alone between scores and products would explain it, by the rows under e9, but no run changes that alone. The 21 matmuls that e9 adds cost 0.22 to 0.26 each.

- **Terms 3 and 4, waits and clock: 23 less 7 forecast, 25.6 measured.** Place by place: head 7 lost 7.5, clock included, by the x load between the two transfers (4.5 forecast, clock apart), as e1 shows. Head 2 lost some 10.6, 5.6 of waits and 5 for 10 us at half clock (8 forecast for heads 2 and 3, and head 3 lost nothing), and its cause was the one named, DVE full of modulation (e2). Head 6 waits 0.4, for 1.5. Head 1 was the wrong wait: not the maxima's trip (7 forecast), but 2.48 for the mixer's first vector part, plus 7 us of half clock that begin 0.5 us into that wait, behind six broadcasts.

  Term 4 gave nothing back, and its 9 us rest on a misread row. In the 25.3 us up to the copy at 344.2 PE ran 13 full scores and 22 products, where a half has 9 and 18; DVE was late with the copy. In the whole of head 0 the kernel before loses 4.4, by 2.0 of waits and 4.9 at half clock. The changed kernel loses 5.1 there, by 0.8 of waits and 8.5 at half clock, to 286.7 us.

  "What a wait does to the clock" was mis-sized too: I took 2 us of loss at two boundaries, and half clock costs 14.1 in the eight heads, not only behind waits (e9, e11). The two longest waits in the heads, 4.79 and 7.02, each have 10.2 us at half clock (392.5 to 402.8 behind the first, 553.0 to 563.2 from within the second), but in e1 a wait of 0.90 stands ahead of products at half speed as well. Behind the 1.81 us in the prediction's row the clock was at half from 334.1 to 337.5, 3.4 us and not some 4.5.

- **At nothing.** The values cost nothing that shows in the new order (e10), but do in the old (e5, 4.4 to 8.1 us at the start). The subtractions on DVE did no harm (e6).

- **The rivals.** (c), the exposed trip, has the right sign and, with 3025, a time nearer than the forecast's. Its mechanism is found at head 7 alone; at heads 1, 5 and 6 the trip is all but covered, and the rest of the loss is made by the work, the clock and DVE. That 3025 is near was luck. (a), covered waits, is the way that e15 goes, but for the 3.6 us that e15 is ahead on the median and not for 24.6, since head 0 keeps its slow start and the work is dearer.

The prediction had the changed kernel's lists and placed its waits by them, so the order is not what it lacked. It lacked the price of the clock and of matmuls among others of another kind. The order matters for the repair: in e2, e3, e4, e11 and e12 a cause that is taken from one head comes back as waits or half clock in another, and of the single steps e1's gain is the only one that stays. Which rule in the scheduler makes the bunches was not isolated; e14 and e15 change several at once.
